# Two prepared feed-forward units: an earlier start, a longer pause behind each load, and high halves stored at the cast

## The chip, the cores and the metric

The kernel runs on one core of one Trainium2 chip. The metric is the device time of one execution in microseconds (us), here the median of three runs. One execution was also recorded by the hardware profiler; engines are named as there: PE (TensorE matmuls), PEld (its weight loads), DVE (VectorE), ACT (ScalarE), POOL (GpSimd), SP (SyncE, which issues most DMAs). L627 means line 627 of the kernel before.

## What is computed

One layer of a hybrid encoder on a sequence of 1024 tokens of width 1024, in float32:

```python
h = rmsnorm(x, norm_mix)
q, k, v, r, lr_f, lr_b, u, g_a, g_b = split(h @ w_in)
o = gla_fwd(q, k, v, ...) + gla_bwd(q, k, v, ...)          # gated linear attention, 4 heads
y_a = (rmsnorm_per_head(o) * gla_norm * silu(r)) @ w_branch_gla
y_b = grouped_linear(multiscale_pool(u)) * pool_scale      # windows 2, 4, 8, 16
x = x + (sigmoid(g_a) * y_a + sigmoid(g_b) * y_b) @ w_out
gate, up = split(rmsnorm(x, norm_ffn) @ w_ffn_in)          # d_ff = 2816
x = x + (silu(gate) * up) @ w_ffn_out
return rmsnorm(x, norm_final)
```

## The kernel before

**Arithmetic.** Each float32 operand is split into a high half, rounded to float32r by a cast on ACT (L198, L627), and a low half, the difference, computed on DVE or POOL (L199, L618). A product of two 128-row operands is then three matmuls (high by high, high by low, low by high); `mm3` (L293) issues such a **triple**. The large matrix products are done by Strassen-like recombination: seven products p = 1 to 7 of sums of blocks instead of eight. Each product in the gate stage is four triples (`product`, L967), written to one PSUM bank.

**The stage around the change** is the gate loop (L1305). It works on ten gate units n = 0 to 9, each a pair of column blocks of w_in; units 0 and 1 give the pool input, 2 to 5 the gate of branch A, 6 to 9 that of branch B. Run n goes through products 1, 5, then product 4 of the unit before, then 6, 2, 3, 7 (`run_of`, L956; the last run ends 2, 7, 3, 4). In this text (n,p) is product p of unit n. Products 1, 6, 7, 4 add up in one PSUM bank, 5 and 3 in another, 2 has its own. After each product an engine takes the bank's content: ACT copies it (products 1, 6, 5: L1265), or DVE adds it to what was copied (2, 3, 7: L1270), or ACT takes the sigmoid straight from the bank (4: L1273). The product that adds onto a bank waits for the copy of the one before it: 6 for the copy of 1, 7 for that of 6, 4 for the add of 7. For units 6 to 9 each finished gate row is multiplied by a pooled product: one more triple into a bank named yb (L1283), three of them after product 7 and one after product 4, from features and weights loaded before (L1207, L1211). The banks of products 5 and 2 and of yb come from one pool of five, so the third yb of a run takes the bank of that unit's product 5 and 3. Weights are split four products ahead (`gates_ahead.step`, L1317: cast wh on ACT, low half wl on POOL, block sums fs on DVE at L902).

**Pacing by hand.** The schedule is manual: the order in which Python issues instructions is the order on each engine and queue. Side work is a generator that `pump` (L159) advances; it is called once per triple with dt = 1 and takes the next step when the cost of the last is used up. `side` holds the pooling mixer (begun in run 2, L1327); `aside` holds block preparation, made by `prepare_beside` (L641).

**The preparation.** `beside` (L605) turns a list of jobs into steps. A job may run an operation on POOL, name a source to be split, or be empty. In each step it first issues the stores put off from the step before (`put` steps), then the low half (DVE) of what was cast in the last step, then the cast (ACT) of the source that was named `lag` steps ago, then the new job. `unit_jobs` (L560) gives the jobs of one of the first two feed-forward units: a step that issues two loads of 512 KB of w_ffn_in on SP into slots, empty steps, then seven sources, four of them behind a POOL sum (in the order 4, 1, 2, 5, 7, 6, 3). Each source's high and low half lie in a ring of five temporary buffers (`t2`) and are stored, 256 KB each, to u_out in DRAM from ACT's queue, from where the feed-forward stage loads them. Before, the high and the low half are stored together, two steps behind the cast. All other loads take one of 39 slots and wait until the slot's last user is done.

The preparation starts at the head of run 7 (L1310 to L1313), with 3.1 triples per step, put 1, lag 2. What is left of it at the head of run 9 is issued at once by `finish_beside` (L1315). `prepare_beside` is also used for the branch, feature and output matrices.

Of the kernel before, what the change touches and what calls it, by code (L numbers as in the profile page):

```python
# [17 lines left out]
P = 128  # L18
# [15 lines left out]
D_FF = 2816  # L34
# [18 lines left out]
def kernel(  # L53
# [20 lines left out]
    nc = tc.nc  # L74
    x, out = x[0], out[0]
    w_in, w_branch, w_out = w_in[0], w_branch_gla[0], w_out[0]
    w_ffn_in, w_ffn_out = w_ffn_in[0], w_ffn_out[0]
# [18 lines left out]
    def slot(dtype=F32, shape=(2, HALF), s="slot"):  # L96
        return slots.tile([P, *shape], dtype, tag="slot", name=name(s))

    def t2(width=HALF, dtype=F32, s="t"):
        return tmp.tile([P, width], dtype, tag="t2", name=name(s), padded_shape=[P, HALF + 2 * PAD])  # L100
# [10 lines left out]
    def as_f32(ap):  # L111
        return ap.bitcast(F32)
# [74 lines left out]
    def begin(gen, delay=0.0):  # L187
        side.append([gen, delay])

    def finish_side():  # L190
        while side:
            for _ in side[0][0]:
                pass
            side.pop(0)
# [325 lines left out]
    READY = 2  # L520
    f_order = [f for q in range(PAIRS) for f in (q, q + PAIRS)]
# [4 lines left out]
        return w[k0 : k0 + 2 * P, c_half * HALF : (c_half + 1) * HALF].rearrange("(k p) c -> p k c", p=P)  # L526


    def loading(srcs, tiles):
        def loads():  # L530
            for t, src in zip(tiles, srcs):
                nc.sync.dma_start(t, src)

        yield loads, None, None
        for _ in range(2):
            yield None, None, None


# [21 lines left out]
    def unit_jobs(n):  # L560
        raw = [slot(F32, (KT, P), "fraw")[:, :, :] for _ in range(2)]
        a11, a12, a21, a22 = (t[:, 4 * j : 4 * j + 4, :].rearrange("p k c -> p (k c)") for t in raw for j in range(2))
        yield from loading(
            [w_ffn_in[:, c0 : c0 + P].rearrange("(k p) c -> p k c", p=P) for c0 in (f_order[n] * P, D_FF + f_order[n] * P)], raw
        )
        for op, p, src in (
            (None, 4, a22), (None, 1, a11), (None, 2, a12), (partial(padd, a22, a21, a22), 5, a22),
            (partial(psub, a21, a11, a21), 7, a21), (partial(psub, a11, a22, a11), 6, a11),
            (partial(psub, a12, a12, a11), 3, a12),
        ):  # L570
            yield op, src, u_out[n][p]
# [28 lines left out]
    def parts_for(src):  # L600
        if len(src.shape) == 2:
            return [t2(dtype=F32R, s=s)[:, :] for s in ("uph", "upl")]
        return [slot(F32R, s=s)[:, :, :] for s in ("trh", "trl")]

    def beside(jobs, every, put, lag, eng):  # L605

        casts, differ = [None] * lag, None
        puts = [[] for _ in range(put)]
        while True:
            job = next(jobs, None)  # L610
            if not any((job, *casts, differ, *puts)):
                return
            for pair in puts.pop(0):
                eng.dma_start(*pair)
            puts.append([])
            if differ:
                src, (hi, lo), dst = differ
                nc.vector.tensor_tensor(lo, src, as_f32(hi), op=ALU.subtract)  # L618
                if len(src.shape) == 2:
                    puts[-1] += [(dst[:, i, :], as_f32(t)) for i, t in enumerate((hi, lo))]  # L620
                else:
                    right.setdefault(dst, []).append((hi, lo))
            differ, cast = None, casts.pop(0)
            if cast:
                src, dst = cast
                parts = parts_for(src)
                nc.scalar.copy(parts[0], src)  # L627
                differ = src, parts, dst
            casts.append(None)
            if job:  # L630
                op, src, dst = job
                if op:
                    op()
                if src is not None:
                    casts[-1] = src, dst
                elif dst is not None:

                    puts[-1].append((dst, op.args[0]))
            yield every

    def prepare_beside(jobs, every, put=PUT, lag=1, eng=nc.sync):  # L641
        aside.append([beside(chain(*jobs), every, put, lag, eng), every])

    def finish_beside():
        while aside:
            for _ in aside[0][0]:
                pass
            aside.pop(0)
# [398 lines left out]
    def pooled(g, u, hi, lo):  # L1047
        width = WINDOWS[g]
        n = HALF + 2 * PAD
        for half in range(2):  # L1050
            s = t2(n, s="ws")
            nc.vector.tensor_tensor(s[:, 1:n], u[half][:, : n - 1], u[half][:, 1:n], op=ALU.add)
            yield 1
            lo_p, hi_p, step = 1, n, 1
            while 2 * step < width:
                a = t2(n, s="ws")
                lo_p, hi_p = lo_p + step, hi_p - step
                nc.vector.tensor_tensor(
                    a[:, lo_p:hi_p], s[:, lo_p - step : hi_p - step], s[:, lo_p + step : hi_p + step], op=ALU.add
                )  # L1060
                yield 1
                s, step = a, 2 * step
            e = slice(PAD, 2 * PAD) if half == 0 else slice(HALF, PAD + HALF)
            nc.vector.tensor_tensor(s[:, e], s[:, e], edge[:, half, g, :], op=ALU.mult)
            body = slice(PAD, PAD + HALF)
            nc.vector.scalar_tensor_tensor(
                s[:, body], s[:, body], 1.0 / width, u[half][:, body], op0=ALU.mult, op1=ALU.subtract
            )
            yield 1
            nc.scalar.copy(hi[:, half, :], s[:, body])  # L1070
            yield 1
            nc.vector.tensor_tensor(lo[:, half, :], s[:, body], as_f32(hi[:, half, :]), op=ALU.subtract)
            yield 0.2
# [13 lines left out]
    def line_make():  # L1087
        n = len(made)
        if n < len(line):
            while len(loads) <= n:  # L1090
                line_load()
            while len(begun_sums) <= n:
                line_sums()
            made.append(line[n][2](loads[n]))
# [124 lines left out]
    def pooling():  # L1219

        for g in range(GROUPS):
            u = [t2(HALF + 2 * PAD, s="u") for _ in range(2)]
            nc.gpsimd.memset(u[0][:, :PAD], 0.0)
            nc.gpsimd.memset(u[1][:, PAD + HALF :], 0.0)
            nc.sync.dma_start(u[0][:, PAD:], u_rows[g][:, : HALF + PAD])
            nc.sync.dma_start(u[1][:, : PAD + HALF], u_rows[g][:, HALF - PAD :])
            yield 4
            hi, lo = slot(F32R, s="ph"), slot(F32R, s="pl")
            for cost in pooled(g, u, hi, lo):
                yield POOLING * cost  # L1230
            nc.scalar.dma_start(p_out[g][0], as_f32(hi[:, :, :]))
            yield 4
            nc.scalar.dma_start(p_out[g][1], as_f32(lo[:, :, :]))
            stored.add(g)
            yield 1
# [69 lines left out]
    for n, run in enumerate(gate_runs):  # L1305
        zs[n] = Gates(n)
        last = n == len(gate_units) - 1
        if n == 0:
            prepare_beside(map(output_jobs, range(4)), 2.8, eng=nc.scalar)
        if n == 7:  # L1310
            finish_side()
            finish_beside()
            prepare_beside(map(unit_jobs, range(READY)), 3.1, 1, 2, nc.scalar)  # L1313
        if last:
            finish_beside()  # L1315
        for at, (of, p) in enumerate(run):
            if not gates_ahead.step() and at in (5, 7):  # L1317
                line_make()
            zs[of].run(p)
            if at in (1, 2) and not last:  # L1320
                gunits[n + 1].load()
            if p in (7, 4):
                zs[of].store(int(p == 4))
            if at == 4:
                flush(nc.scalar)
                if n == 2:
                    begin(pooling(), 4)  # L1327
            if 5 <= n < 9 and at == 5:
                load_pool_weights(n - 5)
            elif n >= 6 and at == 2:  # L1330
                split_pool_weights(n - 6)
            if n >= 6 and at == (0 if last else 3):
                load_pooled(n - 6)
            if last and at == 1:
                load_block(0, 0)
                line_load()
                line_load()
                load_block(1, 0)
            elif last and at == 2:
                line_load()  # L1340
                line_load()
                load_block(0, 1)
                load_block(1, 1)
# [477 lines left out]
    for at, p in enumerate(OUT_ORDER):  # L1821
# [4 lines left out]
        for i in range(CLOSE if closing else n_of):  # L1826
            n = at * n_of + i
# [50 lines left out]
```

## Time and profile before

| | us |
|---|---|
| three runs: lowest, median, highest | 1401.12, 1401.21, 1401.93 |
| the profiled execution, its own time | 1400.29 |
| its span, first to last instruction | 1398.6 |
| PE busy in the span | 1367.3 |
| DVE, POOL, ACT busy | 848.1, 751.1, 624.0 |
| data moved | 243.56 MB, 173 GB/s of HBM traffic over the span |

The span leaves 1.7 us of the profiled execution's time outside. Busy time is summed over instructions; matmuls are pipelined, so one is listed with 0.39 us while the next starts after 0.23. In a timeline a row has start, duration, engine (PE; ACTq and SPq are the DMA queues of ACT and SP), line, operation, output and inputs, and in brackets how long the engine stood idle before it and what ended that wait. In the list of waits a row has who waited for whom, the total, how often, and the longest. A row of a tile's view has the shortest, median and longest duration in ns and the starts of the first and last instruction. In the view by stretches of time each engine has its busy time and instruction count, then the granted clock, the DMA share (1 is all 16 engines busy) and GB/s.

### The profile page before, as it was taken

To read this page: it belongs to the slowest core of one execution; us is meant where nothing else is said; L and a number is where in the kernel's file an instruction comes from. 1 tells how busy PE (TensorE), PEld (TensorE's weight loads), DVE (VectorE), ACT (ScalarE), POOL (GpSimd) and SP (SyncE) were. 2 spreads that over 40 slices of the span, in tenths; PEclk is the share of its full clock that TensorE was granted. 3 is DMA by queue.
4 is the path that set the end of the run, shared out by engine and by line. 5 is a ranking of instruction groups with operands and counts; after the bars stand their busy time and mean duration, and the time that the engine had idled before them with its cause. 6 is when DMAs were issued, how large, how long until landed. Compare 5 with 4: busy or idle time off the path is not lost. (4 is left out here: it accounts for less than half of the span.)

```text
span 1398.6 us, 18511 instructions
## 1 busy us (share of the span) xinstructions
PE 1367.3 (98%) x6654; PEld 1152.5 (82%) x6654; DVE 848.1 (61%) x1073; ACT 624.0 (45%) x1125; POOL 751.1 (54%) x565
## 2 busy tenths in 40 slices
PE   7999999999999999899999999999999999999997
PEld 6889898988888888788887888888888888888876
DVE  6266757667745885587875865556565556343364
ACT  6364655554334444455346633333333334453253
POOL 3261716041387555468665176666666667464364
PEclk9999999999999999999999999999999999999999
DMA  6211423322477668997425455554444447976461
GB/s 191 76 57 50 136 64 103 106 62 75 135 241 234 207 215 270 323 402 275 151 76 183 164 180 173 173 173 159 147 140 148 142 153 254 385 257 216 165 240 62
DMA packets 167453, 243.56 MB, mean 174 GB/s; under 512 B 10905, under 2 KB 97857, under 8 KB 167361
## 3 DMA queue, kind: packets, MB, share of 16 engines
q1 hardware_dynamic: 154944, 216.16, 46.3%
q10 hardware_dynamic: 12416, 26.22, 5.0%
q8 instruction: 52, 0.85, 0.3%
q14 instruction: 41, 0.33, 0.1%
HBM read 164.48 MB, written 77.86 MB: 173 GB/s over the span
## 5 line engine op out<-in xcount | busy, mean ns | idle before, releaser
L199 POOL TENSOR_TENSOR wl<-fs,wh 128x512 fp32r<-128x512 f32 x120 | 165.0, 1379 | 163.9 <-ACT wh L198 141.3
L291 PE MATMUL ps<-gl,wh 128*128 128x512 f32 x616 | 240.0, 390 | 0.8 <-DVE gl L1472 0.8
L291 PE MATMUL ps<-gh,wh 128*128 128x512 f32 x616 | 240.6, 391 | 0.0
L291 PE MATMUL ps<-gh,wl 128*128 128x512 f32 x616 | 239.9, 390 | 0.0
L199 POOL TENSOR_TENSOR wl<-fraw,wh 128x512 fp32r<-128x512 f32 x90 | 129.9, 1443 | 67.2 <-ACT wh L198 66.5
L199 POOL TENSOR_TENSOR ol<-gor,oh 128x1024 fp32r<-128x1024 f32 (+1 forms) x42 | 102.1, 2437 | 91.9 <-ACT oh L198 72.9
L291 PE MATMUL ps<-hh,wh 128*128 128x512 f32 x376 | 149.5, 398 | 0.0
L291 PE MATMUL ps<-hh,wl 128*128 128x512 f32 x376 | 146.8, 391 | 0.0
L291 PE MATMUL ps<-hl,wh 128*128 128x512 f32 x376 | 146.6, 390 | 0.0
L291 PEld LDWEIGHTS ps<-gl,wh 128*128 128x128 f32 x616 | 115.7, 188 | 24.9 <-DVE gl L1472 1.3
L291 PEld LDWEIGHTS ps<-gh,wl 128*128 128x128 f32 x616 | 115.7, 188 | 24.2
L199 POOL TENSOR_TENSOR wl<-raw,wh 128x512 fp32r<-128x512 f32 x44 | 61.4, 1411 | 137.7 <-ACT wh L198 135.2
L291 PEld LDWEIGHTS ps<-gh,wh 128*128 128x128 f32 x616 | 115.7, 188 | 23.6
L291 PE MATMUL ps<-oh,oh 128*128 128x512 f32 x308 | 120.0, 390 | 1.3 <-DVE x L1800 1.3
L291 PE MATMUL ps<-ol,oh 128*128 128x512 f32 x308 | 120.1, 390 | 0.2 <-DVE ol L199 0.2
L291 PE MATMUL ps<-oh,ol 128*128 128x512 f32 x308 | 119.9, 389 | 0.0
L199 POOL TENSOR_TENSOR wl<-wraw,wh 128x512 fp32r<-128x512 f32 x56 | 90.7, 1646 | 46.7 <-ACT wh L198 46.7
L199 DVE TENSOR_TENSOR ol<-wor,oh 128x1024 fp32r<-128x1024 f32 (+1 forms) x42 | 63.9, 1542 | 53.1 <-ACT oh L198 50.0
L198 ACT CAST wh<-fs 128x512 fp32r<-128x512 f32 x120 | 73.8, 615 | 30.8 <-DVE fs L902 23.1
L291 PEld LDWEIGHTS ps<-hh,wl 128*128 128x128 f32 x376 | 70.6, 188 | 15.1
L291 PEld LDWEIGHTS ps<-hl,wh 128*128 128x128 f32 x376 | 70.7, 188 | 13.4
L291 PEld LDWEIGHTS ps<-hh,wh 128*128 128x128 f32 x376 | 70.7, 188 | 13.4
(258 smaller groups left out, 3173.2 us busy)
## 6 DMA issues: line engine op xcount, KB each, us to landing
fraw<-in_w_ffn_in_dram SPq DMA_DIRECT2D x44, 512.0 KB, 6.4
gor<-g_out SPq DMA_DIRECT2D x35, 512.0 KB, 7.0
raw<-in_w_in_dram SPq DMA_DIRECT2D x48, 256.0 KB, 4.4
g_out<-s SPq DMA_DIRECT2D x44, 256.0 KB, 2.3
fraw<-in_w_in_dram SPq DMA_DIRECT2D x20, 512.0 KB, 4.2
wor<-t_out SPq DMA_DIRECT2D x20, 512.0 KB, 7.6
g_out<-g SPq DMA_DIRECT2D x33, 256.0 KB, 2.6
x<-in_x_dram SPq DMA_DIRECT2D x16, 512.0 KB, 3.9
```

The costliest lines, as they stand in the source:

```text
L198: nc.scalar.copy(hi, src)
L199: eng.tensor_tensor(lo, src, as_f32(hi), op=ALU.subtract)
L291: nc.tensor.matmul(ps, a[i], b[j], start=first and n == 0, stop=last and n == 2, skip_group_check=onto)
```

## The change

Three things change for these two units, and a fourth with them:

- The preparation starts in run 6 behind its fifth product, (6,2), behind the stores that are issued there, and no longer at the head of run 7. `finish_side` and `finish_beside` move with it.
- A step costs 2.7 triples instead of 3.1, and a source is cast one step behind its job instead of two (lag 1).
- Four empty steps follow a unit's loads instead of two.
- The high half's store is issued on ACT right behind its cast; only the low half's is put off. This holds for two-dimensional sources, which only these units have.

```diff
-    def loading(srcs, tiles):
+    def loading(srcs, tiles, blank=2):
...
-        for _ in range(2):
+        for _ in range(blank):
             yield None, None, None
...
         yield from loading(
-            [w_ffn_in[:, c0 : c0 + P].rearrange("(k p) c -> p k c", p=P) for c0 in (f_order[n] * P, D_FF + f_order[n] * P)], raw
+            [w_ffn_in[:, c0 : c0 + P].rearrange("(k p) c -> p k c", p=P) for c0 in (f_order[n] * P, D_FF + f_order[n] * P)], raw, 4
         )
...
                 if len(src.shape) == 2:
-                    puts[-1] += [(dst[:, i, :], as_f32(t)) for i, t in enumerate((hi, lo))]
+                    puts[-1].append((dst[:, 1, :], as_f32(lo)))
...
                 nc.scalar.copy(parts[0], src)
+                if len(src.shape) == 2:
+                    eng.dma_start(dst[:, 0, :], as_f32(parts[0]))
                 differ = src, parts, dst
...
-        if n == 7:
-            finish_side()
-            finish_beside()
-            prepare_beside(map(unit_jobs, range(READY)), 3.1, 1, 2, nc.scalar)
...
                 if n == 2:
                     begin(pooling(), 4)
+                if n == 6:
+                    finish_side()
+                    finish_beside()
+                    prepare_beside(map(unit_jobs, range(READY)), 2.7, 1, 1, nc.scalar)
```

## Prediction

> **What bounds the kernel now.** I read the page first, then the waits of TensorE, then the timelines of PE, ACT, DVE and SP from 505 to 600 us, where the trace shows the casts and stores that the change touches.
>
> ```profile
> span 1398.6 us, 18511 instructions
> PE 1367.3 (98%) x6654; PEld 1152.5 (82%) x6654; DVE 848.1 (61%) x1073; ACT 624.0 (45%) x1125; POOL 751.1 (54%) x565
> ...
> PE ps L291 <- ACT ga L1265: 3.8, 1, 3.8
> ...
> PE ps L291 <- DVE dl L163: 0.7, 1, 0.7
> ...
> PE yb L291 <- DMA pl<-p_out: 0.3, 1, 0.3
> ```
>
> PE is busy for 98% of the span, so work is worth something only where PE waits. The fourth line is one of its longest single waits: once, for 3.8 us, an ACT copy of a PSUM bank (L1265) was late. Its place, on PE and on ACT:
>
> ```profile
> 573.65 0.40 PE L291 MATMUL yb<-ph,wpl 128*128 128x512 f32 x1
> 577.82 0.79 PE L291 MATMUL ps<-trh,wh 128*128 128x512 f32 x1 [3.77 <-ACT ga L1265]
> ...
> 580.86 0.40 PE L291 MATMUL ps<-trl,wh 128*128 128x512 f32 x1
> 581.09 0.40 PE L291 MATMUL ps<-trh,wl 128*128 128x512 f32 x1
> ```
> ```profile
> 564.79 0.62 ACT L627 CAST uph<-fraw 128x512 fp32r<-128x512 f32 x1 [1.59 <-issue]
> ...
> 567.27 0.62 ACT L627 CAST uph<-fraw 128x512 fp32r<-128x512 f32 x1 [0.82 <-DMA u_out<-upl]
> ...
> 573.77 0.62 ACT L627 CAST uph<-fraw 128x512 fp32r<-128x512 f32 x1 [1.24 <-DMA u_out<-upl]
> ...
> 575.70 0.93 ACTq L614 DMA_DIRECT2D u_out<-upl  x1
> 576.67 0.62 ACT L198 CAST wh<-fraw 128x512 fp32r<-128x512 f32 x1 [2.28 <-DVE ga L1243]
> 577.19 0.58 ACT L1265 COPY ga<-ps 128x512 f32<-128x512 f32 x1
> ```
>
> The copy at 577.19 belongs to product 1 of run 9, (9,1) from here on, and stands in ACT's queue behind the last casts and stores of the second prepared unit. PE wants its bank again two products later. So this wait is made by the preparation. In the stretch from 480 to 600 us its casts wait for low stores and its low halves for high stores:
>
> ```profile
> DVE upl L618 <- DMA u_out<-uph: 8.6, 5, 2.9
> ...
> ACT uph L627 <- DMA u_out<-upl: 6.6, 5, 1.8
> ```
>
> **What the stall costs.** Undisturbed spacing first:
>
> ```profile
> 529.58 0.39 PE L291 MATMUL ps<-trh,wh 128*128 128x512 f32 x1
> ...
> 540.48 0.40 PE L291 MATMUL yb<-ph,wph 128*128 128x512 f32 x1
> ...
> 541.88 0.40 PE L291 MATMUL yb<-ph,wph 128*128 128x512 f32 x1
> ```
>
> From 529.58 to 540.48 lie four products of 12 matmuls: 10.90 / 48 = 0.227 us each, 0.68 us per triple, 2.72 us per product. From 573.65 to 581.09 nine matmuls start; 9 x 0.227 = 2.04 us would do, 7.44 us were used: **5.4 us lost**. Of this 3.94 us is the gap (577.82 - 573.65 - 0.23) and 1.45 us slow matmuls after it, seven at about 0.43 us. On this the Trainium skill (TensorE: Matmul & The Clock Gate, Part 1: The HAM clock gate) states that the clock falls to half after an idle window of about 3.4 us and needs such a window of work to return; by that page the second part would be up to 1.7 us, an estimate, and the sum 0.25 us larger. The rows agree in kind and their 1.45 us is used.
>
> A smaller loss stands at 563:
>
> ```profile
> 562.34 0.40 PE L291 MATMUL yb<-ph,wph 128*128 128x512 f32 x1
> 563.02 0.50 PE L291 MATMUL yb<-pl,wph 128*128 128x512 f32 x1 [0.29 <-DMA pl<-p_out]
> 563.36 0.39 PE L291 MATMUL yb<-ph,wpl 128*128 128x512 f32 x1
> 563.60 0.39 PE L291 MATMUL yb<-ph,wph 128*128 128x512 f32 x1
> ```
>
> Three matmuls take 1.26 us instead of 0.70: **0.56 us**, for a load of pooled features that came late.
>
> **Start and pace.** Pacing counts triples. Before, 64 triples lie between the start of run 7 and that of run 9 (two runs of 28, eight pooled triples); the 24 steps (20 jobs, then lag 2, low half and store) need 24 x 3.1 = 74.4, so 20 are issued in step and L1315 issues the last four at once: two casts, three low halves, eight stores. After, 11 triples more (two products and three pooled triples of run 6) make 75, and 27 steps (24 jobs, then cast, low half, store) need 72.9. All is issued by triple 73, two triples before L1315, which then finds nothing. This removes the burst ahead of the copy: -5.4 us. At the new place (behind L1327, in run 6) the pooling generator has spent 4 + 4 x 9 + 1.75 x (6.4 + 8.4 + 10.4 + 12.4) = 106 units of cost against 112 triples passed, so finish_side forces nothing.
>
> **Loads.** Their slots decide:
>
> ```profile
> 512.78 2.94 SPq L532 DMA_DIRECT2D fraw<-in_w_ffn_in_dram  x2
> ...
> 531.02 8.43 SPq L532 DMA_DIRECT2D fraw<-in_w_ffn_in_dram  x2
> ...
> 551.95 1.78 DVE L902 TENSOR_TENSOR fs<-fraw,fraw 128x512 f32<-128x512 f32 x1
> ...
> 553.79 0.34 SPq L1207 DMA_DIRECT2D ph<-p_out  x1
> ```
>
> The first load ran 8 us before PE reached run 7 and still waited for slots; between its old and new place no slot is taken, so I keep it at 512.78 to 515.7. The same holds for the second (531 to 539.5). On SP each moves past one pool-weight load (L1211), which then goes out behind it, near 516 and 540; its cast stands in ACT's order behind the pooled triple of (n-1,4), PE at 529.58 and one run of 32 triples later at 551.4. Over 11 us for 128 KB: nothing. The pooled load at 553.79 waited for a DVE sum that ended at 553.73, and DVE was late behind low halves of unit 0. After, those low halves stand 11 to 14 triples (7 to 10 us) earlier in the order, so this load should come some us sooner and its 0.56 us go; if not, they stay.
>
> **Casts, low halves, stores.** Their number is the same; their density is not: 2.7 x 0.68 = 1.84 us per step instead of 2.11, and the high store waits on ACT for its cast, 0.6 us in which ACT issues nothing else. (The two landing lines: high stores, then low stores.)
>
> ```profile
> L627 ACT CAST uph<-fraw x14: 614/622/628, 533.5 to 573.8; 128x512 fp32r<-128x512 f32 x14
> L618 DVE TENSOR_TENSOR upl<-fraw,uph x14: 676/692/1791, 536.4 to 574.5; 128x512 fp32r<-128x512 f32 x14
> ...
> L633 POOL TENSOR_TENSOR fraw<-fraw,fraw x4: 1277/1296/1754, 541.0 to 567.8; 128x512 f32<-128x512 f32 x4
> ...
> DMA to landing us min/median/max: 2.1/2.6/2.9
> ...
> DMA to landing us min/median/max: 2.9/3.9/4.9
> ```
> ```profile
> 529.08 0.60 ACT L1273 ACTIVATE ga<-ps 128x512 f32<-128x512 f32 x1 [1.62 <-PE ps L291]
> 529.87 0.62 ACT L198 CAST wh<-fs 128x512 fp32r<-128x512 f32 x1
> 530.57 1.29 POOL L199 TENSOR_TENSOR wl<-fs,wh 128x512 fp32r<-128x512 f32 x1 [1.74 <-ACT wh L198]
> 535.97 1.19 ACTq L498 DMA_DIRECT2D yb_out<-ga  x2
> ```
>
> The ring has five buffers, so cast i waits for the low store of cast i-3, issued one step before it (3.9 us median landing, 2.6 if alone like the high ones). Walking the first unit from these rows: first low store 530.0; Pool's product-5 sum behind the wl at 530.57 runs 531.9 to 533.3; fourth cast 533.3 to 533.9, so the copy of (7,6) ends near 535.3, and PE wants it at 529.58 + 3 x 2.72 = 537.7: 2.4 us spare. Fifth cast 535.3 to 536; the store pair of L498 takes 1.2 us; sixth cast, behind Pool's next sum and the third low store (535.2 + 2.6 to 3.9), 538.3 to 539.4. DVE queues its low half (0.7) and then the add of (7,3) (0.7) behind that cast, so this add ends 540.5 to 541.5. It frees the bank that the third pooled triple of the run takes, at 541.88: 0.4 to 1.4 us spare. I take no new stall, as the median rows give one in no place; the cover is ACT's waiting for PE (the 1.62 us in the row at 529.08). The bound: a low half of 1.79 us instead of 0.69 ends the add near 542.6, a stall of 0.7 us; with a landing of 4.9 us as well about 1.7. The second unit has the same geometry, so 0 to 3.4 us in all. A gain here is excluded: none of it feeds PE.
>
> **Sum.** Profiled run 1400.29 - 5.4 - 0.56 = 1394.3. The median of before is 0.92 above that run: **1395.3 us**.
>
> **Rivals.** (1) The denser steps make the add of (n,3) late at the third pooled triple, with the terms above: 1395.3 + 0.7 to 3.4, at the middle 1397.3. For it: the small spare. Against: before, the add of (8,3) ended as close to its third pooled triple (564.30), and PE did not wait:
>
> ```profile
> 563.14 0.68 DVE L1270 TENSOR_TENSOR ga<-ps,ga 128x512 f32<-128x512 f32 x1
> ```
>
>  A wait of 0.29 us (above) left the next spacing at 0.24 to 0.34, so such waits cost about their own length.
>
> (2) The branch stage gives it back, because its loads and not PE set its pace:
>
> ```profile
> 600.00:610.00 10.00, 10.00 (x45) 8.27 (x45) 9.28 (x5) 6.82 (x11) 8.47 (x4) 1.00 1.03 411
> ```
>
> The DMA engines are full there (share 1.03). If loads do not come earlier, PE arrives 5.96 us too soon and up to all of it returns: 1401.2; half of it 1398.2. Against: PE does not wait in this row, eight stores (2 MB, about 5 us at 411 GB/s) leave the stretch just before, and slots come free sooner. The Trainium skill (Trainium Kernel Development and Optimization, Key Constraints) says that transfers issued from SP and ACT share the same 16 engines; earlier stores then delay loads at 526 to 545.
>
> (3) Slower: low stores land so late in both units that ACT falls behind them as it did in the burst. The fourth cast waits for the store issued at 530.0, the third low store goes out some 2.4 us behind that cast's start, and the sixth cast waits for it: it starts at 532.4 + 2L for a landing L, and the add ends 2.0 us later (cast 0.6, low half 0.7, add 0.7). Break-even is 3.0 us of stall per unit, the add ending at 544.9, thus L = 5.2 us. At L = 6 us the stall is 4.5 us, and 1.45 of slow matmuls behind it, per unit: 1395.3 + 11.9 = 1407.2. The highest landing of a low store was 4.9.
>
> (4) The preparation is still unfinished at run 9 (a miscount of some triples): 1401.2 or a little less.
>
> **Chances.** Forecast 0.66, with its own range 1394.1 (the 0.7 us wait on dl gone too, and half of the spread of before, 0.4) to 1396.5; rival (1) 0.18, of which 0.04 above 1398.4; (2) 0.09, of which 0.05 above 1398.4; (3) 0.05; (4) 0.02. About 0.2% (2.8 us) is what a measurement can tell from no change. Faster: 0.66 + 0.14 + 0.04 = 0.84; same 0.04 + 0.05 + 0.02 = 0.11; slower 0.05. The range takes in the forecast's own and rival (1) up to its bound, 1395.3 + 3.4: 1394.1 to 1398.7, which leaves out some 0.14.
>
> **What would show it.** Right: no PE wait on ga L1265 near 574, no slow matmuls behind it, the last cast (L627) before 567, no DVE low half waiting for a high store. Wrong: a PE wait on ga L1270 or on a yb bank near 542 or 564, ACT waits on u_out<-upl far over 6.6 us in sum, or PE waits on dl or wh between 590 and 650.

## The result and the profile after

| us | before | after |
|---|---|---|
| median | 1401.16 (6 runs, 1400.32 to 1401.93) | 1396.19 (6 runs, 1395.15 to 1396.89) |
| profiled execution | 1400.29 | 1396.31 |
| its span | 1398.6 | 1394.6 |

The ratio is 0.9965, interval 0.9953 to 0.9978: the changed kernel is 4.97 us faster. In the same comparison made again on another chip (r1_after_again) it was 1396.35 against 1400.61, ratio 0.9970 [0.9959, 0.9981]. In the changed kernel the cast is still L627, its store is L629, and what lies below has line numbers higher by two: the PSUM copy is L1267 and the add L1272.

The head of the page of the changed kernel:

```profile
span 1394.6 us, 18506 instructions
...
PE 1367.8 (98%) x6654; PEld 1154.2 (83%) x6654; DVE 847.5 (61%) x1073; ACT 624.4 (45%) x1125; POOL 752.2 (54%) x565
```

TensorE has the same work, so the 4.0 us of span are waits and slow matmuls that went. Where, is told by one row of each trace: the pooled triples' first matmuls, whose first and last start (in us, behind the durations in ns) bracket the last three triples of run 6 and the gate runs 7 to 9. Before, after, and the changed kernel with six ring buffers (an experiment below):

```profile
L291 PE MATMUL yb<-ph,wph x16: 393/398/399, 518.6 to 595.0; 128*128 128x512 f32 x16
```
```profile
L291 PE MATMUL yb<-ph,wph x16: 392/398/399, 518.9 to 591.1; 128*128 128x512 f32 x16
```
```profile
L291 PE MATMUL yb<-ph,wph x16: 392/400/404, 517.7 to 588.3; 128*128 128x512 f32 x16
```

The stretch took 76.4 us before, 72.2 after, and 70.6 in the third kernel, in which TensorE waits nowhere in it. So 70.6 is what its matmuls need, 5.8 us were lost before and 1.6 are lost after. All that went lies in this stretch: what lies outside it took 1322.2 us before and 1322.4 after (span less stretch).

The wait at 574 us and the slow matmuls behind it are gone. What is left is a new wait on TensorE, here in its timeline; the three pooled matmuls at the end, which had waited for pl before, now follow each other at 0.23:

```profile
559.83 0.39 PE L291 MATMUL ps<-hh,wl 128*128 128x512 f32 x1
561.49 0.50 PE L291 MATMUL ps<-trh,wh 128*128 128x512 f32 x1 [1.28 <-ACT ga L1267]
561.83 0.40 PE L291 MATMUL ps<-trl,wh 128*128 128x512 f32 x1
562.06 0.40 PE L291 MATMUL ps<-trh,wl 128*128 128x512 f32 x1
562.30 0.40 PE L291 MATMUL ps<-trh,wh 128*128 128x512 f32 x1
...
564.37 0.40 PE L291 MATMUL yb<-ph,wph 128*128 128x512 f32 x1
564.60 0.39 PE L291 MATMUL yb<-pl,wph 128*128 128x512 f32 x1
564.83 0.40 PE L291 MATMUL yb<-ph,wpl 128*128 128x512 f32 x1
```

From 559.83 to 562.30 lie four matmuls, 2.47 us where 4 x 0.227 = 0.91 would do: 1.56 us lost. It is (8,7) waiting for the copy of (8,6). ACT's timeline shows why that copy was late:

```profile
553.04 0.36 ACTq L629 DMA_DIRECT2D u_out<-uph  x1
...
559.84 0.62 ACT L627 CAST uph<-fraw 128x512 fp32r<-128x512 f32 x1 [4.45 <-DMA u_out<-uph]
...
560.86 0.58 ACT L1267 COPY ga<-ps 128x512 f32<-128x512 f32 x1 [0.40 <-ACT uph L627]
```

The fourth cast of the second unit stood 4.45 us at the head of ACT's queue, until a high half stored two casts earlier had left its buffer, and the copy, whose product had long been done, stood behind it. The chain of waits puts that store on the path, 6.71 us from its issue to its landing:

```profile
553.04 6.71 DMA u_out<-uph
```

In the list of waits the roles are swapped against before: casts now wait mostly for high stores and low halves for low ones.

```profile
ACT uph L627 <- DMA u_out<-uph: 6.3, 3, 4.5
...
DVE upl L618 <- DMA u_out<-upl: 5.8, 4, 3.0
```

And the stores take longer from issue to landing (high, then low; medians 2.6 and 3.9 before). These lines rest on few stores: of the 14 of each kind the view has a landing for two high and three low ones here, and for three and two before.

```profile
DMA to landing us min/median/max: 3.2/4.2/5.3
...
DMA to landing us min/median/max: 2.5/5.5/7.3
```

More stores can be timed by the cast or low half that waited for them, from the store's issue to the start of that instruction. Before, these are ten, with 2.2 to 5.0 us; after, eight, with 4.7 to 7.4 us. One of before, a high store that held a low half until 4.15 us after its issue:

```profile
562.60 0.92 ACTq L614 DMA_DIRECT2D u_out<-uph  x1
```
```profile
566.75 1.63 DVE L618 TENSOR_TENSOR upl<-fraw,uph 128x512 fp32r<-128x512 f32 x1 [2.93 <-DMA u_out<-uph]
```

The DMA engines are fuller in these microseconds. The last three columns are the granted clock, the DMA share and GB/s, before and then after:

```profile
520.00:542.00 22.00, 22.00 (x98) 18.16 (x97) 9.25 (x13) 9.46 (x18) 10.47 (x8) 1.00 0.78 242
```
```profile
520.00:542.00 22.00, 22.00 (x98) 18.13 (x97) 14.02 (x16) 10.35 (x19) 13.58 (x11) 1.00 0.93 305
```

### The profile page after: what moved, and what is told of

The parts are those of the page before. It is cut to its first block, busy times and chain, and to the rows that moved or that the text cites. A ratio compares the mean times of both kernels' runs of the same rounds, so it can differ in the third digit from the quotient of the medians.

```text
span 1394.6 us, 18506 instructions
## 1 busy us (share of the span) xinstructions
PE 1367.8 (98%) x6654; PEld 1154.2 (83%) x6654; DVE 847.5 (61%) x1073; ACT 624.4 (45%) x1125; POOL 752.2 (54%) x565
## 4 chain that ended last, share of the span: by engine, by line
PE 66%; DVE 4%; issue 3%; DMA 3%; POOL 3%; ACT 2%; ACTq 0%; SPq 0%; POOLq 0%; DVEq 0%
PE ps L291 63%; POOL wl L199 1%; DMA wor<-t_out 1%; DMA u_out<-uph 1%; DMA fraw<-in_w_ffn_in_dram 1%; PE yb L291 1%; PE tp L994 1%; DMA u_out<-upl 0%; PE op L835 0%; DVE x L1558 0%; DVE ws L1054 0%; ACT wh L198 0%; POOL n3rs L1541 0%; POOL mg L1185 0%; POOL gl L1474 0%
## 5 line engine op out<-in xcount | busy, mean ns | idle before, releaser
L291 PEld LDWEIGHTS ps<-hh,wl 128*128 128x128 f32 x376 | 70.6, 188 | 15.0
L291 PEld LDWEIGHTS ps<-hl,wh 128*128 128x128 f32 x376 | 70.8, 188 | 13.4
L291 PEld LDWEIGHTS ps<-hh,wh 128*128 128x128 f32 x376 | 70.7, 188 | 13.4
```

Of the source, the lines that this page charges most:

```text
L291: nc.tensor.matmul(ps, a[i], b[j], start=first and n == 0, stop=last and n == 2, skip_group_check=onto)
```

## The experiments

Two theories were set against each other. **A: the burst.** What costs is the four left-over steps that L1315 issued at once ahead of the copy of (9,1); a schedule that leaves none over has its 5 us. **C: store landing.** What costs is the ring of five buffers: casts on ACT and low halves on DVE stand in order ahead of the copies and adds that free PSUM banks, and wait until an earlier store has landed; the burst is only the place where such waits pass the slack. Further views, B and D, are told where an expectation names them. A and C both have this change faster. They differ on each edit alone, on the ring's size, and on a denser schedule.

For each kernel the table gives the stretch as read above, what it lost over 70.6, and the longest waits of TensorE in it.

| kernel | ring | stretch | lost | longest waits of TensorE | median | ratio [interval] |
|---|---|---|---|---|---|---|
| before | 5 | 76.4 | 5.8 | 3.8 ga (copy) | 1400.1 to 1401.2 | 1 |
| after | 5 | 72.2 | 1.6 | 1.3 ga (copy) | 1396.19 | 0.9965 [0.9953, 0.9978] |
| e1_start_only | 5 | 73.8 | 3.2 | 3.0 ga (copy) | 1398.81 | 0.9989 [0.9980, 0.9997] |
| e3_pace_only | 5 | 75.8 | 5.2 | 2.8 ga (add) | 1400.03 | 0.9996 [0.9986, 1.0007] |
| e2_all_but_start | 5 | 76.9 | 6.3 | 4.2 ga (copy) | 1400.69 | 0.9996 [0.9986, 1.0005] |
| e6_pairs | 5 | 74.8 | 4.2 | 1.9 ga (add) | 1400.33 | 0.9999 [0.9990, 1.0008] |
| e9_ring_four | 4 | 75.9 | 5.3 | 1.8 ga (add) | 1401.78 | 1.0008 [0.9999, 1.0017] |
| e8_four_small | 5 | 72.7 | 2.1 | 1.3 ga (copy) | 1396.37 | 0.9972 [0.9963, 0.9982] |
| e7_six_buffers | 6 | 70.6 | 0 | none | 1395.07 | 0.9958 [0.9945, 0.9971] |
| b6_before_six | 6 | 71.4 | 0.8 | 0.5 ga (copy) | 1395.70 | 0.9964 [0.9951, 0.9977] |
| e3_six | 6 | 70.6 | 0 | none | 1395.67 | 0.9969 [0.9957, 0.9980] |
| e1_six | 6 | 70.7 | 0.1 | none | 1396.45 | 0.9973 [0.9963, 0.9982] |

What lies outside the stretch took 1320.8 to 1323.6 us in all of them, without order; stretches are of one profiled execution, medians of 5 to 12 (6 to 33 for the kernel before). In e9_ring_four and e6_pairs the profiled executions, 1398.45 and 1398.69, were among their fastest, so their medians lost more than the table's 5.3 and 4.2.

The sum of what casts and low halves wait for stores between 480 and 600 us does not order these kernels: with 8.8 us e2_all_but_start loses 6.3, with 14.3 us e1_six loses 0.1. What counts is whether work that TensorE needs stands behind such a wait.

**The start alone** (e1_start_only): the kernel before, with these lines moved from run 7 to run 6, at the old pace, lag and pause.

```diff
-        if n == 7:
-            finish_side()
-            finish_beside()
-            prepare_beside(map(unit_jobs, range(READY)), 3.1, 1, 2, nc.scalar)
...
+                if n == 6:
+                    finish_side()
+                    finish_beside()
+                    prepare_beside(map(unit_jobs, range(READY)), 3.1, 1, 2, nc.scalar)
```

> The kernel before with one part of the change: the preparation starts in run 6 behind its fifth product; pace 3.1, lag 2, two empty steps and paired stores stay. Its 24 steps then need 74.4 of 75 triples, so nothing is left for the head of run 9. Theory A (the gain is the burst of left-over steps ahead of the copy of (9,1), nothing else): the 3.8 us wait near 574 is gone, 1395.5 to 1397. Rival B (the gain comes from the high halves stored at the cast or the shorter lag): the wait stays, 1400 to 1402.

Measured: 1398.81 (1396.57 to 1402.83). The wait at 574 went, and one of 3.01 us came at (8,7), on TensorE and then on ACT:

```profile
563.83 0.50 PE L291 MATMUL ps<-trh,wh 128*128 128x512 f32 x1 [3.01 <-ACT ga L1265]
```
```profile
562.67 0.62 ACT L627 CAST uph<-fraw 128x512 fp32r<-128x512 f32 x1 [5.02 <-DMA u_out<-upl]
```

The place is the one of the changed kernel's wait, the cause of the same kind: a cast stood 5.02 us for a low store. With no burst, over half of the loss stayed. Against A.

**The pace alone** (e3_pace_only): the kernel before with a denser schedule, which also leaves no step over.

```diff
-            prepare_beside(map(unit_jobs, range(READY)), 3.1, 1, 2, nc.scalar)
+            prepare_beside(map(unit_jobs, range(READY)), 2.6, 1, 2, nc.scalar)
```

> The kernel before with a pace of 2.6 triples per step instead of 3.1 and nothing else: 24 steps need 62.4 of 64 triples, so no burst, without an earlier start. Theory A: the wait near 574 is gone or under 1 us, 1396 to 1398. Rival B: 1400 to 1402. If the denser steps cost by themselves (rival 1 of the prediction), new PE waits stand between 545 and 575 and the time is 1398 to 1400.

Measured: 1400.03 (1397.83 to 1403.77), no difference from the kernel before that can be told. The waits of casts on low stores rose from 6.6 to 13.4 us, and (8,4) was held by the add of (8,7) on DVE:

```profile
576.41 0.50 PE L291 MATMUL ps<-trh,wh 128*128 128x512 f32 x1 [2.77 <-DVE ga L1270]
```

The burst is removed and 5.2 of 5.8 us remain. A falls as a full account.

**All but the start** (e2_all_but_start): the changed kernel, the start back at the head of run 7.

```diff
+        if n == 7:
+            finish_side()
+            finish_beside()
+            prepare_beside(map(unit_jobs, range(READY)), 2.7, 1, 1, nc.scalar)
...
-                if n == 6:
-                    finish_side()
-                    finish_beside()
-                    prepare_beside(map(unit_jobs, range(READY)), 2.7, 1, 1, nc.scalar)
```

> The changed kernel with its start put back to the head of run 7; pace 2.7, lag 1, four empty steps and high stores at the cast stay. 27 steps need 72.9 triples, 64 are there: 23 steps are issued in step, the last four (two casts, three low halves, six stores) at once at the head of run 9. Theory A: a PE wait of 2 to 4 us on the copy of (9,1) is back, 1398.5 to 1401. Rival B: as fast as the changed kernel, 1396 plus or minus 0.7.

Measured: 1400.69 (1396.70 to 1402.66). The burst is back and with it the wait on the copy of (9,1), 0.4 us longer than before, and slow matmuls behind it:

```profile
578.70 0.80 PE L291 MATMUL ps<-trh,wh 128*128 128x512 f32 x1 [4.19 <-ACT ga L1267]
579.29 0.63 PE L291 MATMUL ps<-trl,wh 128*128 128x512 f32 x1
```

So a burst does make such a wait in a ring of five, and the ring has its part in it: the last low half stood 2.70 us for a low store, and two low stores and then the copy stood behind it in ACT's queue.

```profile
576.41 0.69 DVE L618 TENSOR_TENSOR upl<-fraw,uph 128x512 fp32r<-128x512 f32 x1 [2.70 <-DMA u_out<-upl]
```

With the start at run 7, where steps are left over, the other edits gain nothing. This run puts back the late start and the burst together and does not part them.

**Both halves stored together** (e6_pairs): the changed kernel, the high half's store put off again to stand beside the low half's.

```diff
-                    puts[-1].append((dst[:, 1, :], as_f32(lo)))
+                    puts[-1] += [(dst[:, i, :], as_f32(t)) for i, t in enumerate((hi, lo))]
...
-                if len(src.shape) == 2:
-                    eng.dma_start(dst[:, 0, :], as_f32(parts[0]))
```

> The changed kernel with both halves stored together one step behind the low half, as before; all else as changed. Theory A: within 1 us of the changed kernel, 1395.2 to 1397.2. Rival B (the early high store frees the ring's buffers and matters): casts wait longer for stores, the wait of 1.3 us at 561 grows to 3 us or more, 1398 to 1400.

Measured: 1400.33 (1398.69 to 1403.35): the high halves' earlier store is worth about 4 us inside this change. The time lies just above what B gave, but its wait of 3 us did not come; the longest is 1.90 us, on an add that stood on DVE behind a low half that had waited 2.14 us for a high store. Waits on stores, from the list:

```profile
DVE upl L618 <- DMA u_out<-uph: 15.6, 8, 4.2
...
ACT uph L627 <- DMA u_out<-upl: 10.7, 4, 4.4
ACT uph L627 <- DMA u_out<-uph: 7.7, 2, 5.4
```

Together 34.0 us, against 13.8 in the changed kernel (6.3, 5.8 and 1.7). A store that goes out one step later gives its buffer back one step later, with the same start, pace and pause, and no burst. For C.

**The ring: six, five, four.** The buffer that e7 adds takes its room from the small buffers, four of them for five; e8 does only that and keeps the ring, as a control; e9 has a ring of four. b6, e3_six and e1_six give six buffers to the kernel before (burst and all), to e3 and to e1.

```diff
-    tmp = ctx.enter_context(tc.tile_pool(name="tmp", bufs=5))
+    tmp = ctx.enter_context(tc.tile_pool(name="tmp", bufs=6))
...
-        return small.tile([P, *shape], F32, tag="s1", name=name(s))
+        return small.tile([P, *shape], F32, tag="s1", name=name(s), bufs=4)
...
-        wpool[g] = [small.tile([P, 2 * P], F32R, tag="s1", name=name(s)) for s in ("wph", "wpl")]
+        wpool[g] = [small.tile([P, 2 * P], F32R, tag="s1", name=name(s), bufs=4) for s in ("wph", "wpl")]
```

The changed kernel once more, beside them on the same chip:

> The changed kernel itself, to stand beside the others on one chip. 3.5 to 5.5 us below the kernel before; one new PE wait of 1 to 3 us between 545 and 575 in its profile.

Measured: 1396.35, the wait at (8,7) again, 1.23 us.

> The changed kernel with six buffers instead of five in the ring that holds the high and low halves; the room comes from one of the five small buffers of the attention and pool weights. Theory C (the gain that the removed burst should give is partly lost to casts and low halves that wait for a buffer whose store has not landed): waits of L627 and L618 on u_out fall to under half of their 14 us in sum, the PE wait near 561 is gone, 0.5 to 1.5 us below the changed kernel. Rival D (they wait for POOL or for the issue of DMAs, not for buffers): the PE wait stays, same time within 0.7 us.

Measured: 1395.07 (1393.53 to 1396.05), the lowest median of this study, with no wait of TensorE in the stretch. Its stores land no faster: the three that a cast or low half still waited for took 7.1 to 7.5 us. They only hold nobody up for long (2.4 us of such waits against 13.8): the cast that stood 4.45 us for a store now waits for its POOL sum and starts at 556.43.

```profile
556.43 0.62 ACT L627 CAST uph<-fraw 128x512 fp32r<-128x512 f32 x1 [2.91 <-POOL fraw L635]
```

> Control for the six-buffer kernel: the changed kernel with four instead of five small buffers and the ring at five. Expected within 0.7 us of the changed kernel, or up to 2 us slower if the attention needs the fifth.

Measured: 1396.37 (1395.52 to 1401.95), the wait of 1.34 us at (8,7) in place. The four small buffers do nothing; the sixth ring buffer does it.

> The kernel before with six buffers in the ring (and four small ones), burst and all. Theory C: the burst's casts wait less, the PE wait near 574 falls from 3.8 to 1.5 to 3 us, 1 to 3.5 us below the kernel before. Theory A in its strict form (the number of instructions in the burst is what counts): the wait stays at 3 us or more, at most 1 us below.

Measured: 1395.70 (1394.58 to 1396.97), as much as the whole change. The burst is still there, its last stores go out right ahead of run 9's first cast and copy, and the copy of (9,1) follows at 573.48 instead of 577.19:

```profile
571.98 0.93 ACTq L614 DMA_DIRECT2D u_out<-upl  x1
572.95 0.62 ACT L198 CAST wh<-fraw 128x512 fp32r<-128x512 f32 x1 [1.88 <-PE ps L291]
573.48 0.58 ACT L1265 COPY ga<-ps 128x512 f32<-128x512 f32 x1
```
```profile
574.11 0.50 PE L291 MATMUL ps<-trh,wh 128*128 128x512 f32 x1 [0.48 <-ACT ga L1265]
```

Of the 3.77 us on that copy 0.48 stay, which is what the burst costs when none of its casts waits more than 0.3 us for a store. Both the wait and the time fell further than C had said (1.5 to 3 us, and 1 to 3.5 below the kernel before). That is decisive against A in its strict form and for C.

> The changed kernel with four instead of five temporary buffers in the ring (and four small buffers, as in the run with four small buffers alone). Store landing (C): a cast or low half now waits for a store one buffer younger, so the waits of ACT and DVE on stores between 480 and 600 us grow from 6 and 5 us to over 15 each, and PE waits on copies or adds (ga) for 3 us or more in at least one unit: 1399 to 1406 us. Left-over burst (A): there is no burst in this kernel, whatever the ring, so the time stays at 1396.4 within 1 us.

Measured: 1401.78 (1398.39 to 1403.97), 5 us slower than the changed kernel, though the waits on stores (12.9 and 1.8 on ACT's casts, 9.9 on DVE) fell short of the 15 each, and the single waits of TensorE of the 3 us. The nine stores that a cast or low half waited for took 4.4 to 7.2 us, no longer than in the changed kernel (4.7 to 7.4): fewer buffers, not slower stores, made the loss.

> The kernel before with 2.6 instead of 3.1 triples per step, and six ring buffers. With five buffers this pace gave 1400.0 us, with a PE wait of 2.8 us at 576. Store landing (C): with six that wait is under 0.5 us and the time 1395 to 1396.5, as the kernel before with six. Left-over burst (A) with the ring's gain lying in another stage: the wait of 2.8 us stays and the time is 1397.5 or more.

Measured: 1395.67 (1393.45 to 1397.20). The 2.77 us wait is gone.

> The kernel before with the start in run 6, and six ring buffers. With five buffers the start alone gave 1398.8 us, with a PE wait of 3.0 us at 564. Store landing (C): no PE wait over 0.5 us between 500 and 600, time 1394.5 to 1396. If the start needs the other edits for another reason than the ring (B): the wait at 564 stays over 2 us and the time is 1397 or more.

Measured: 1396.45 (1395.03 to 1398.19), 0.45 above the bound; the 3.01 us wait is gone. The list of TensorE's waits from 500 to 600 us has the same single line for e3_six and e1_six; it stands at 507 and 506, ahead of the stretch and of the preparation's first cast (what was expected of e1_six had no wait over 0.5 us from 500 on):

```profile
PE ps L291 <- DVE ga L1270: 1.0, 1, 1.0
```

With six buffers start and pace are free to choose within the measurement: the four kernels lie between 1395.07 and 1396.45, in intervals that overlap.

## Why the prediction was right, and where it was not

- **The stall of 5.4 us on the copy of (9,1) goes:** right, in place and in size (the stretch without it and without the late load needs 5.8 us less than before). That the stretch shrank by 4.2 us and not by 5.4 + 0.56 is due to the new stall, two points below.
- **"This removes the burst ahead of the copy":** the burst is removed, but it was not the whole cause. Removing it by the pace alone gained 0.6 us in the stretch (76.4 to 75.8), by the start alone 2.6; leaving it and adding a buffer gained 5.0. The change needs both the earlier start and the high store at the cast: with either taken out (e2, e6) no gain can be measured. That the high store works by giving buffers back sooner fits e6's waits; that the earlier start works by giving the stores time is a reading, since e2 also brings back the burst.
- **"I take no new stall, as the median rows give one in no place": the step that failed.** A stall of 1.56 us stands at (8,7). The working took the landings of before, 2.6 and 3.9 us at the median, which rest on three and two stores, where the stores that held something up took 4.7 to 7.4 us in the changed schedule. Even before, such stores took up to 5.0 us, and a high store 4.15 us (shown above), beyond the 2.9 us that the view has as the longest. The first unit still shows the walk's order: its fourth cast came at 534.18 (walked: 533.3), the copy of (7,6) began at 535.20 (walked to end near 535.3), the sixth cast at 541.09 (walked: 538.3 to 539.4).
- **The tight place:** wrong. The walk put it at the add of (n,3), said to free the third pooled triple's bank with 0.4 to 1.4 us to spare. In the first unit this add ran from 543.34, after TensorE had started that triple, which did not wait:

```profile
542.13 0.40 PE L291 MATMUL yb<-ph,wph 128*128 128x512 f32 x1
```
```profile
543.34 0.68 DVE L1272 TENSOR_TENSOR ga<-ps,ga 128x512 f32<-128x512 f32 x1
```

 So the third pooled triple did not need the bank of products 5 and 3, against what is said of the banks ahead of the prediction, and the tight place was the copy of (n,6), which had been given 2.4 us of slack. In the second unit the fourth cast alone ate that slack. Rival (1) had the sort of loss and a range that holds its size (0.7 to 3.4 us), at the wrong bank; the measured time, 1396.19, lies in its range as well as in the forecast's own.
- **The ring's order:** cast i waits for the low store of cast i-3 held before (6.6 us on low stores) and failed after, where the wait shown above is on the high store of cast i-2. A likely reason is that, with stores at different steps, the buffers are handed back in another order; the traces leave buffer numbers out, so this is not shown.
- **Loads:** as said. The first is at its old place, the second near 531, each ahead of a pool-weight load; the pooled load of 553.79 comes 1.8 us sooner, and its 0.56 us are gone. SP's timeline:

```profile
513.01 2.98 SPq L532 DMA_DIRECT2D fraw<-in_w_ffn_in_dram  x2
516.04 0.58 SPq L1213 DMA_DIRECT2D wpr<-in_w_pool_group_dram  x1
...
530.24 10.13 SPq L532 DMA_DIRECT2D fraw<-in_w_ffn_in_dram  x2
540.43 1.23 SPq L1213 DMA_DIRECT2D wpr<-in_w_pool_group_dram  x1
...
551.98 0.53 SPq L1209 DMA_DIRECT2D ph<-p_out  x1
```

- **The preparation ends before run 9:** right in order: the copy of (9,1) runs at 572.21 instead of 577.19, with no burst ahead of it. In time it ended later than said: the last cast ran at 568.86 and not before 567, by the 1.9 us that it waited for its POOL sum. Rival (4) is out. One low half still waited for a high store, 1.7 us, where none was to.
- **Rival (2), the branch stage gives it back:** out. TensorE is busy throughout, at full clock, with the DMA engines full as before:

```profile
600.00:610.00 10.00, 10.00 (x46) 8.29 (x45) 7.44 (x5) 4.75 (x8) 5.33 (x4) 1.00 1.03 418
```

- **Rival (3), slower by late low stores:** its condition, a landing above 5.2 us, came true (of the eight stores timed above six took 5.6 us or more), and its result did not. It counted on the sixth cast waiting for two low stores one behind the other; in the changed kernel casts waited for high stores. The wait of 1.28 us is the same mechanism in small, and e9 shows it at 5 us.
- **The sum:** 1394.3 for the profiled execution, which took 1396.31: 2.0 too low, of which 1.56 is the new stall. The 0.92 us then added came from three runs, against a single profile; over 19 to 33 runs in later comparisons the kernel before had medians of 1400.13 to 1400.86, near its profiled 1400.29. The one error hid half of the other, so that the forecast came within 0.9 us of the median is in part luck.

What stays open: why stores land later in the changed kernel. The DMA share rose with it (0.78 to 0.93 between 520 and 542 us), but no run took traffic away to test that. (The 6.71 us of the store at 553.04 do not contradict the 5.3 us that its tile's view has as the longest landing: the view has none for this store.) Also open is whether a sixth buffer takes the loss from e2_all_but_start and e6_pairs too, to which none was given.

## What to carry to other kernels

When work prepared on the side goes through a small ring of buffers to DRAM, count which store each write into the ring waits for, and what stands behind that write on its in-order engine: one buffer more was worth as much here (5 us) as moving the start, the pace, the pause and the stores. A burst that ends just before a stall need not be its cause; removing it alone only moved the wait to the next tight copy or add. Do not take landing times from the old schedule into a denser one, and ask how many transfers stand behind a median.

## What the hardware showed

**A wait under 2 us can cost the clock, and one of 3 us need not.** In e6_pairs TensorE waited 1.90 us; 1.5 us later its matmuls slowed to one per 0.43 us for about 3 us:

```profile
550.72 0.50 PE L291 MATMUL ps<-trh,wh 128*128 128x512 f32 x1 [1.90 <-DVE ga L1270]
...
552.26 0.63 PE L291 MATMUL ps<-trh,wh 128*128 128x512 f32 x1
552.69 0.63 PE L291 MATMUL ps<-trl,wh 128*128 128x512 f32 x1
553.12 0.63 PE L291 MATMUL ps<-trh,wl 128*128 128x512 f32 x1
```

The view by stretches gives a granted clock of 0.71 there:

```profile
550.00:555.00 5.00, 4.28 (x13) 3.40 (x14) 4.36 (x8) 4.02 (x8) 2.69 (x2) 0.71 0.77 225
```

In e9_ring_four a wait of 1.81 us did the same (clock 0.70). The waits of 3.01 us in e1_start_only and 2.77 us in e3_pace_only were followed by no slow matmul, those of 3.77 (before) and 4.19 (e2) by several. On this the Trainium skill (TensorE: Matmul & The Clock Gate, Part 1: The HAM clock gate) says that the clock halves after at least one idle window of about 3.4 us, and that this window runs freely. The two short waits disagree with the length of idleness that it asks for, and here the measurement decides; a window that runs freely and trips on too little work, not only on none, would allow all six cases, but no run here tests where the windows lie. So a short wait can cost twice its length: e6 lost 4.2 us with 2.1 us of waits.
